# Hybrid encoder layer on one core: roots through memory, attention outputs one step later, another order in the MLP's head

## The chip, the core and the metric

The kernel runs on one core of a Trainium2 chip. Its time is the device time of one execution in microseconds (us). TensorE (PE) multiplies and transposes, VectorE (DVE), ScalarE (ACT) and GpSimd (POOL) do elementwise work, and transfers are issued from the queues of SyncE (SP) and ACT.

## The reference

The input is 1024 tokens by 1024 features. All arithmetic is in float32.

```python
hn = rmsnorm(h, norm_mix[l])
proj = jnp.einsum('bsd,de->bse', hn, w_in[l])
qa, ka, va, qb, kb, vb = jnp.split(proj, splits, axis=-1)
...
o_a = window_gqa_sink(qa, ka, va, sink[l])        # |i-j| <= 128, 8 heads, 2 key heads
o_b = neighbourhood_attention(qb, kb, vb, rpb[l]) # 8 x 16 windows on a 16 x 64 grid, 8 heads
mix = jnp.concatenate([rmsnorm(o_a, norm_a[l]), rmsnorm(o_b, norm_b[l])], axis=-1)
h = h + jnp.einsum('bse,ed->bsd', mix, w_out[l])
hn = rmsnorm(h, norm_ffn[l])
h = h + conv_gated_mlp(hn, w_gate[l], w_up[l], conv_w[l], conv_b[l], w_down[l])
return rmsnorm(h, norm_final)
```

## The kernel before

Features lie on the 128 partitions and tokens along the free dimension. Every float32 operand of a product is split into a rounded part (`hi`, made by ACT) and a remainder (`lo`, made by DVE as a subtraction), and a product is three matmuls: hi by hi, hi by lo, lo by hi. Roundings of weights are `whi` and `wlo`; of probabilities `ph` and `pl`; of the MLP's operands `hg`.

The program has four stretches. Up to about 57 us it computes the first three column tiles of the projection. Then two streams are interleaved by hand on PE: the attention's units (first 16 of the window attention, two groups of key heads times 8 blocks of tokens; then 32 of the grid attention, 8 heads times 4), and as filler the blocks of the remaining projections and of the first half of the output projection (`rest`, jobs 0 to 22, each of 16 blocks). A table of places, `aux[job, block]`, puts the norm of the first attention into the filler. After the attention come the second half of the output projection and the MLP, whose first four gate and up units ("the head") overlap the norm before it; then the rest of the MLP, the down product and the final norm.

PE's order is the order of the code. The order of the other engines is set by a list scheduler; `high_priority` pulls an instruction forward, and `behind(names)` keeps it after the last instruction that was recorded under these names: "high" is the latest `ph`, "rest" the latest `pl`, "narrow" the latest reciprocal of a norm.

Places that the change touches:

- `t_step` transposes probabilities into a bank `pt` and splits them; `v_step`, one step later, multiplies them with the values into the bank `o`. After the last one of a unit or of half a head, `leave` copies one half of the partitions of `o` into `ot` (ACT, L491 or L574) and adds it to the other half into `mix` (DVE, L495 or L576), at once.
- `square_a`, `narrow_a`, `wide_a`, `normed_a` are the norm of the first attention's output. `narrow_a` leaves 1024 reciprocal roots as `v`, 128 partitions by 8 columns. `wide_a`, at `aux[12, 11]` and `aux[12, 13]`, spreads each half of them over all partitions by four PE transposes (`widen`, L236) into a `pj` bank and copies it to `rstda` with ACT (L851). `normed_a` multiplies (DVE, L855, eight instructions).
- `OutA.run` adds the residual to a finished bank of the output projection (L659).
- In the MLP's head, `pure(f)` loads and rounds a gate weight, `settle_out` adds squares for the norm (L1069), and `head_weights(i, "s2")` forms a difference of weights (L1083). `p1`, `p2` and `p5` of a unit multiply into the banks `x`, `z` and `y`; a `join` (L1084) empties `z`. The units 2 and 3 use for `z` the two banks that the units 0 and 1 use for `y`.

Of the kernel before, what the change touches and what calls it, by code (L numbers as in the profile page):

```python
# [20 lines left out]
KT = D // 128  # L21
# [37 lines left out]
def hybrid_layer(tc, xT, w_first, w_in, w_out, w_gate, w_up, w_down, small, sink, rpb, consts, rope, out):  # L59
    nc = tc.nc  # L60
    with ExitStack() as ctx:
# [7 lines left out]
        tpool = inner("temps", 3)  # L69
        apool = inner("att", 2)  # L70
        spool = inner("stats", 6)

        slots = {"xg": 16, "op": 14, "mix": 8, "rstd": 1}

# [6 lines left out]
        def bank(name, tag):  # L81
            return psum.tile([128, HALF], F32, name=name, tag=tag)
# [319 lines left out]
                return lpool.tile([128, 2, 386], F32, name="p", tag="mix", bufs=slots["mix"], padded_shape=[128, 2, 512])  # L402
            return apool.tile([128, 2, 386], F32, name="p", tag="p", bufs=5, padded_shape=[128, 2, 392])

        deferred = []

        def exponentials(*order):
            while deferred:
                with tc.high_priority(offset=50):
                    deferred.pop(0)(*order)  # L410
# [39 lines left out]
        def unit_window(g, b):  # L450

            cs, n = near(b), 128 * len(near(b))
            ps4 = [None] * 4
            mask = w2(cst[:, K_MA + 128 * (cs[0] - b + 1):K_MA + 128 * (cs[-1] - b + 2)])
            st = {}

            def q_step(j):
                def go():
                    if j % 2 == 0:
                        st["p"] = pair_tile(True)  # L460
                    ps, _ = scores(qa[g, j // 2][j % 2], ka[g], b)
                    softmax(st, j % 2, ps, n, mask, nsink[:, 4 * g + j - j % 2:4 * g + j - j % 2 + 2])
                    ps4[j] = st["p"][:, j % 2, :]
                return go

            def t_step(i):
                def go():
                    if i == 0:
                        st["o"] = bank("o", "o")
                    pt = bank("pt", "pt")  # L470
                    for j in range(4):
                        nc.tensor.transpose(pt[:, j * 128:(j + 1) * 128], ps4[j][:, i * 128:(i + 1) * 128], ident)  # L472
                    ph, pl = split_pt(pt, HALF)
                    exponentials("high")

                    def v_step():
                        o, v = st["o"], va[g]
                        nc.tensor.matmul(o, v[:, cs[i], :], mv(ph[:, :]), start=i == 0, stop=False)
                        nc.tensor.matmul(o, v[:, cs[i], :], mv(pl[:, :]), start=False, stop=i == len(cs) - 1)
                        if i == len(cs) - 1:  # L480
                            leave()
                    return v_step
                return go

            def leave():
                ot = apool.tile([128, 2, 128], F32, name="ot", tag="ot", bufs=1, padded_shape=[128, 4, 128])
                o4 = pv(st["o"][:, :])
                halved = lambda ap: ap.rearrange("p (s w) -> p s w", s=2)
                for e in range(2):
                    me, other = slice(64 * e, 64 * e + 64), slice(64 - 64 * e, 128 - 64 * e)  # L490
                    nc.scalar.activation(ot[me].rearrange("p j (s w) -> p j s w", s=2), o4[other, e::2], AF.Copy)  # L491
                    for i in range(2):
                        if mix[2 * g + i] is None:
                            mix[2 * g + i] = big("mixa", "mix")
                        nc.vector.tensor_tensor(halved(mix[2 * g + i][me, b * 128:(b + 1) * 128]), o4[me, e + 2 * i], halved(ot[me, i, :]), op=ALU.add)  # L495

            return [q_step(j) for j in range(4)], [t_step(i) for i in range(len(cs))]

# [19 lines left out]
        def units_grid(h):  # L518
# [21 lines left out]
            def t_step(c):  # L540
                def go():
                    if c == 0:
                        st["o"] = [bank("o", "o") for _ in range(2)]
                    bs = near(c)
                    pt = bank("pt", "pt")
                    for i, b in enumerate(bs):
                        at = near(b).index(c) * 128
                        nc.tensor.transpose(pt[:, i * 128:(i + 1) * 128], ps4[b][:, at:at + 128], ident)
                    ph, pl = split_pt(pt, 128 * len(bs))

                    def v_step():
                        for half in range(2):
                            inb = [b for b in bs if b // 4 == half]
                            if not inb:
                                continue
                            lo, hi = (inb[0] - bs[0]) * 128, (inb[-1] - bs[0] + 1) * 128
                            dst = st["o"][half][:, (inb[0] % 4) * 128:(inb[-1] % 4 + 1) * 128]
                            final = c == (4 if half == 0 else NB - 1)
                            nc.tensor.matmul(dst, vb[h][:, c, :], mv(ph[:, lo:hi]), start=not st["begun"][half], stop=False, skip_group_check=True)
                            nc.tensor.matmul(dst, vb[h][:, c, :], mv(pl[:, lo:hi]), start=False, stop=final, skip_group_check=True)  # L560
                            st["begun"][half] = True
                            if final:
                                leave(half)
                    return v_step
                return go

            def leave(half):
                i = 4 + h // 2
                if mix[i] is None:
                    mix[i] = big("mixb", "mix")  # L570
                ot = apool.tile([128, HALF], F32, name="ot", tag="ot", bufs=1)
                w = lambda ap: ap.rearrange("p (b r c s) -> p b s r c", s=2, r=ROWS // 2, c=8)
                o = st["o"][half]
                nc.scalar.activation(ot[me], o[other], AF.Copy)  # L574
                dst = mix[i][me, :].rearrange("p (s r b c) -> p b s r c", s=2, b=NB, c=8)[:, 4 * half:4 * half + 4]
                nc.vector.tensor_tensor(dst, w(o[me, :]), w(ot[me, :]), op=ALU.add)  # L576

            chunks = [[0], [1, 2], [3, 4], [5, 6, 7]]
            return [([q_step(2 * i), q_step(2 * i + 1)], [t_step(c) for c in chunks[i]]) for i in range(4)]
# [56 lines left out]
        class OutA:  # L636
# [12 lines left out]
            def run(self):  # L649
                d = self.d  # L650
                h1[d] = big("h1", "mix" if d < 4 else "op")
                xt = tmp("xr")
                with behind(*["stacked"] * (d > 0)):
                    nc.sync.dma_start(xt, xT[d])
                for h in range(2):
                    ps = bank("pj", "pj")
                    yield from product(ps, self.w, mg[0:4], h)
                    with tc.high_priority(offset=500):
                        nc.vector.tensor_tensor(sv(h1[d][:, tsl(h)]), pv(ps[:, :]), sv(xt[:, tsl(h)]), op=ALU.add)  # L659

            def post(self):
# [180 lines left out]
                if h == 1:  # L842
                    inverse_root(norm["v"], 512)

        def wide_a(h):
            def go():
                if h == 0:
                    live["op"] += 1
                    norm["a"] = big("rstda", "op")
                with tc.high_priority(offset=500):  # L850
                    nc.scalar.activation(norm["a"][:, tsl(h)], widen(norm["v"][:, 4 * h:4 * h + 4], "pj"), AF.Copy)  # L851
            return go

        def normed_a(i, h):
            return lambda: nc.vector.scalar_tensor_tensor(  # L855
                mix[i][:, tsl(h)], mix[i][:, tsl(h)], col(C_NA + i), norm["a"][:, tsl(h)], op0=ALU.mult, op1=ALU.mult)

        aux[11, 8], aux[12, 2], aux[12, 5], aux[12, 11], aux[12, 13] = square_a, narrow_a, narrow_a, wide_a(0), wide_a(1)
        for i in range(8):
            aux[13, 1 + i + i // 2] = normed_a(*divmod(i, 2))  # L860
        aux[1, KEYS] = second_k
        filler = rest()
        live["op"] = sum(needs(m) for m in range(3))
# [102 lines left out]
            nc.scalar.activation(warm, eps, AF.Sqrt)  # L966
        fill(2)
        pend()


        last = tmp("sq")
# [75 lines left out]
        def operand(src, tag):  # L1047

            t = big("hg", tag, F32R)
            nc.scalar.activation(t[:, 0:HALF], src, AF.Copy)  # L1050
            nc.vector.tensor_tensor(t[:, HALF:S], src, f32(t[:, 0:HALF]), op=ALU.subtract)
            return t[:, 0:HALF], t[:, HALF:S]


# [5 lines left out]
        def settle_out():  # L1060
# [5 lines left out]
            with tc.high_priority(offset=500):  # L1066
                nc.scalar.activation(s2, at(d, h), AF.Square)
                if total[h] is not None:
                    nc.vector.tensor_tensor(s2, s2, total[h], op=ALU.add)  # L1069
            total[h] = s2  # L1070

        def normed(h, wide, ds):
# [16 lines left out]
        def head_weights(i, name):  # L1089
# [3 lines left out]
                nc.vector.tensor_tensor(t, u[:, 0:4], u[:, 4:8], op=ALU.add)  # L1093
            elif name == "s2":
                g = load_half(w_gate[f, :, 0:4])
                sub(t, t, g)
            elif name == "s4":
                g = load_half(w_gate[f, :, 4:8])
                sub(t, g, t)
# [170 lines left out]
        units = [Gated(f, *(("s", "o", "pj"), ("pj", "pt", "o"))[i // 2]) for i, f in enumerate(FO[:HEAD])]  # L1270
        units[0].p1()
        units[1].p1()
        pure(FO[2])
        units[0].p2()
        v = inverse_narrow([total[1]], D, "pt")
        units[1].p2()
        wide = widen(v, "pt")
        normed(1, wide, K1)
# [405 lines left out]
```

## Time and profile before

| | |
|---|---|
| median of three runs | 1016.34 us (1015.89 to 1016.55) |
| the profiled execution's own time | 1016.91 us |
| its span, first to last instruction | 1015.1 us |
| outside of the span | 1.8 us |
| granted TensorE clock | 0.998 |
| PE, DVE, ACT, POOL busy | 99%, 82%, 55%, 10% of the span |

The profiled execution is 0.57 us above the median. Busy shares are means over stretches of different kinds; PE's counts a matmul from its start to its modelled end, and matmuls overlap, so the distance between two starts is what a matmul costs in a dense stretch.

### The profile page before, as it was taken

The numbers are of one execution on the slowest core, as the hardware profiler recorded it, in microseconds if no ns is written. First come the engines' busy times: TensorE is split into PE (matmuls) and PEld (weight loads), VectorE is DVE, ScalarE is ACT, GpSimd is POOL, SyncE is SP. The second block draws the span as 40 slices with busy tenths as digits, with TensorE's granted clock in tenths as the row PEclk, the third lists the DMA queues.
The fourth block names the chain that finished last, engine by engine and source line by source line (L and its number), as shares of the span: only waits on it lengthen the run. The fifth ranks groups of instructions, "written<-read, shape, count | busy, mean of one in ns | idle before, by whom it ended". The sixth has DMA issues, their size and how long they took to land.

```text
span 1015.1 us, 14835 instructions
## 1 busy us (share of the span) xinstructions
PE 1006.3 (99%) x5086; PEld 890.2 (88%) x5086; DVE 832.7 (82%) x1566; ACT 561.8 (55%) x1081; POOL 104.0 (10%) x188
## 2 busy tenths in 40 slices
PE   9999999999999999999999999999999999999996
PEld 8899898899899888888888888888888888888886
DVE  7989887768888799999987786786777678986775
ACT  8567776658687554565544443444443645544451
POOL 0224342222232100000000000000000000000002
PEclk9999999999999999999999999999999999999999
DMA  8223122333334366231542233323232699866644
GB/s 295 83 74 92 34 73 63 83 83 83 84 93 135 126 203 222 73 104 63 203 180 100 98 115 114 104 94 131 88 135 88 227 345 322 297 226 231 226 153 166
DMA packets 68220, 144.94 MB, mean 143 GB/s; under 512 B 8240, under 2 KB 18736, under 8 KB 68144
## 3 DMA queue, kind: packets, MB, share of 16 engines
q1 hardware_dynamic: 58208, 118.88, 36.5%
q10 hardware_dynamic: 9936, 25.11, 6.4%
q8 instruction: 40, 0.66, 0.3%
q14 instruction: 36, 0.29, 0.1%
HBM read 103.58 MB, written 28.57 MB: 130 GB/s over the span
## 4 chain that ended last, share of the span: by engine, by line
PE 99%; DVE 1%; issue 0%; ACT 0%; DVEq 0%; POOL 0%; POOLq 0%
PE pj L179 8%; PE pj L181 8%; PE pj L180 8%; PE x L1045 7%; PE x L1043 7%; PE x L1044 7%; PE dn L1045 7%; PE dn L1044 7%; PE dn L1043 7%; PE s L393 4%; PE y L1045 4%; PE y L1043 4%; PE y L1044 4%; PE pt L472 2%; PE z L1043 2%; PE z L1045 2%
## 5 line engine op out<-in xcount | busy, mean ns | idle before, releaser
L1043 PE MATMUL x<-hg,whi 128*128 128x512 f32 x352 | 133.5, 379 | 0.0
L1044 PE MATMUL x<-hg,whi 128*128 128x512 f32 x352 | 133.4, 379 | 0.0
L1045 PE MATMUL x<-hg,wlo 128*128 128x512 f32 x352 | 133.4, 379 | 0.0
L1043 PE MATMUL dn<-xd,whi 128*128 128x512 f32 (+1 forms) x330 | 120.8, 366 | 0.0
L1044 PE MATMUL dn<-xd,whi 128*128 128x512 f32 (+1 forms) x330 | 120.5, 365 | 0.0
L1045 PE MATMUL dn<-xd,wlo 128*128 128x512 f32 (+1 forms) x330 | 120.5, 365 | 0.0
L1017 ACT ACTIVATE whi<-ws 128x512 fp32r<-128x512 f32 (+1 forms) x100 | 60.7, 621 | 74.1 <-DVE ws L1153 14.7
L432 ACT ACTIVATE p<-p,nm 128x385 f32<-128x385 f32 (+3 forms) x128 | 75.1, 587 | 47.0 <-DVE nm L424 44.1
L179 PE MATMUL pj<-xgh,whi 128*128 128x512 f32 x245 | 99.7, 407 | 0.1
L436 POOL TENSOR_SCALAR p<-p,sm 128x384 f32<-128x384 f32 (+1 forms) x128 | 75.6, 603 | 196.0 <-DVE sm L434 179.9
L180 PE MATMUL pj<-xgl,whi 128*128 128x512 f32 x245 | 92.9, 379 | 0.0
L181 PE MATMUL pj<-xgh,wlo 128*128 128x512 f32 x245 | 92.9, 379 | 0.0
L1017 ACT ACTIVATE whi<-raw 128x512 fp32r<-128x512 f32 (+1 forms) x102 | 60.9, 610 | 50.1 <-PE x L1044 15.4
L1018 DVE TENSOR_TENSOR wlo<-ws,whi 128x512 fp32r<-128x512 f32 (+1 forms) x100 | 66.7, 683 | 19.1 <-ACT whi L1017 18.8
L447 DVE TENSOR_TENSOR pl<-pt,ph 128x384 fp32r<-128x384 f32 (+2 forms) x108 | 63.3, 586 | 17.4 <-ACT ph L446 16.3
L1043 PEld LDWEIGHTS x<-hg,whi 128*128 128x128 f32 x352 | 66.5, 189 | 9.5
L1045 PEld LDWEIGHTS x<-hg,wlo 128*128 128x128 f32 x352 | 66.5, 189 | 9.4
L1044 PEld LDWEIGHTS x<-hg,whi 128*128 128x128 f32 x352 | 66.5, 189 | 9.4
L1504 POOL TENSOR_TENSOR h<-h,wide 128x256 f32<-128x256 f32 (+1 forms) x6 | 5.4, 916 | 669.8 <-ACT wide L1500 669.8
L1018 DVE TENSOR_TENSOR wlo<-raw,whi 128x512 fp32r<-128x512 f32 (+1 forms) x102 | 66.7, 670 | 7.0 <-ACT whi L1017 6.8
L446 ACT ACTIVATE ph<-pt 128x384 fp32r<-128x384 f32 (+2 forms) x108 | 55.3, 512 | 25.8 <-PE pt L472 14.4
L1045 PEld LDWEIGHTS dn<-xd,wlo 128*128 128x128 f32 x330 | 62.5, 189 | 7.7
(267 smaller groups left out, 2507.6 us busy)
## 6 DMA issues: line engine op xcount, KB each, us to landing
xd<-x SPq DMA_DIRECT2D x77, 256.0 KB, 4.9
raw<-in_w_down_dram SPq DMA_DIRECT2D x72, 256.0 KB, 4.5
raw<-in_w_gate_dram SPq DMA_DIRECT2D x22, 512.0 KB, 3.5
raw<-in_w_up_dram SPq DMA_DIRECT2D x22, 512.0 KB, 3.7
x<-c ACTq DMA_DIRECT2D x22, 512.0 KB, 2.8
raw<-in_w_in_dram SPq DMA_DIRECT2D x30, 256.0 KB, 2.7
raw<-in_w_down_dram SPq DMA_DIRECT2D x36, 192.0 KB, 4.4
x<-t ACTq DMA_DIRECT2D x11, 512.0 KB, 2.6
```

Source lines behind the costliest of these rows:

```text
L179: nc.tensor.matmul(ps, w[0], mv(x[0][:, tsl(h)]), start=first, stop=False)
L180: nc.tensor.matmul(ps, w[0], mv(x[1][:, tsl(h)]), start=False, stop=False)
L181: nc.tensor.matmul(ps, w[1], mv(x[0][:, tsl(h)]), start=False, stop=last)
L432: nc.scalar.activation(p[:, j, 0:e], p[:, j, 0:e], AF.Exp, bias=nm, scale=-1.0, accum_out=sm[:, j:j + 1])
L436: mark["scaled"] = nc.gpsimd.tensor_scalar(p[:, i, 0:m], p[:, i, 0:m], sm[:, i:i + 1], 1.0, op0=ALU.mult, op1=ALU.mult)
L446: mark["high"] = nc.scalar.activation(ph[:, 0:n], ps[:, 0:n], AF.Copy)
L447: mark["rest"] = nc.vector.tensor_tensor(pl[:, 0:n], ps[:, 0:n], f32(ph[:, 0:n]), op=ALU.subtract)
L1017: nc.scalar.activation(hi, src, AF.Copy)
L1018: nc.vector.tensor_tensor(lo, src, f32(hi[:, :, :]), op=ALU.subtract)
L1043: nc.tensor.matmul(ps, w[0], x[0], start=first and i == 0, stop=False, skip_group_check=True)
L1044: nc.tensor.matmul(ps, w[0], x[1], start=False, stop=False, skip_group_check=True)
L1045: nc.tensor.matmul(ps, w[1], x[0], start=False, stop=last and i == len(ws) - 1, skip_group_check=True)
```

## The change

The first attention's reciprocal roots no longer go through eight PE transposes. One transpose turns `v` into 8 rows of 128, ACT copies them out of the bank, a transfer writes them (4 KB) to a tile in device memory, and a second transfer, five blocks later in the code, reads them back into all 128 partitions of `rstda` (512 KB). Both are issued on ACT's queue. The eight multiplications move four blocks later, and each stays behind the latest `pl`.

`leave` is no longer called at once but put into a list, which the next `t_step` empties after it has split its probabilities, behind its "high" and "rest". `OutA`'s addition stays behind "rest" too.

In the MLP's head `pure(FO[2])` stands after `units[0].p2()` and the norm's root in the code, the differences "s2" stay behind "narrow", and the last addition of squares stays behind the latest rounding of an operand.

```diff
+        spread_pool = ctx.enter_context(tc.tile_pool(name="roots", bufs=1, space=bass.MemoryType.DRAM))
+        roots = spread_pool.tile([8, 128], F32, name="roots")
...
+        def leave_all(*order):
+            while leaving:
+                leaving.pop(0)(order)
...
                     exponentials("high")
+                    leave_all("high", "rest")
...
                         if i == len(cs) - 1:
-                            leave()
+                            leaving.append(leave)
...
-            def leave():
+            def leave(order):
...
+                with behind(*order):
+                    for e in range(2):
+                        me, other = slice(64 * e, 64 * e + 64), slice(64 - 64 * e, 128 - 64 * e)
+                        nc.scalar.activation(ot[me].rearrange("p j (s w) -> p j s w", s=2), o4[other, e::2], AF.Copy)
...
                     ph, pl = split_pt(pt, 128 * len(bs))
+                    leave_all("high", "rest")
...
-                                leave(half)
+                                leaving.append(lambda order, half=half: leave(half, order))
...
-                    with tc.high_priority(offset=500):
+                    with tc.high_priority(offset=500), behind("rest"):
                         nc.vector.tensor_tensor(sv(h1[d][:, tsl(h)]), pv(ps[:, :]), sv(xt[:, tsl(h)]), op=ALU.add)
...
-        def wide_a(h):
+        def row_a():
+            ps, row = bank("row", "pj"), norm["sq"][0:8, 0:128]
+            nc.tensor.transpose(ps[0:8, 0:128], norm["v"], ident)
+            with tc.high_priority(offset=500):
+                nc.scalar.activation(row, ps[0:8, 0:128], AF.Copy)
+                nc.scalar.dma_start(roots, row)
+
+        def wide_a():
+            live["op"] += 1
+            norm["a"] = big("rstda", "op")
+            with tc.high_priority(offset=500):
+                nc.scalar.dma_start(norm["a"], bass.AP(tensor=roots.tensor, offset=roots.offset, ap=[[0, 128], [1, S]]))
+
+        def normed_a(i, h):
             def go():
-                if h == 0:
-                    live["op"] += 1
-                    norm["a"] = big("rstda", "op")
-                with tc.high_priority(offset=500):
-                    nc.scalar.activation(norm["a"][:, tsl(h)], widen(norm["v"][:, 4 * h:4 * h + 4], "pj"), AF.Copy)
+                with behind("rest"):
+                    nc.vector.scalar_tensor_tensor(
+                        mix[i][:, tsl(h)], mix[i][:, tsl(h)], col(C_NA + i), norm["a"][:, tsl(h)], op0=ALU.mult, op1=ALU.mult)
...
-        aux[11, 8], aux[12, 2], aux[12, 5], aux[12, 11], aux[12, 13] = square_a, narrow_a, narrow_a, wide_a(0), wide_a(1)
+        aux[11, 8], aux[12, 2], aux[12, 5], aux[12, 10], aux[12, 15] = square_a, narrow_a, narrow_a, row_a, wide_a
         for i in range(8):
-            aux[13, 1 + i + i // 2] = normed_a(*divmod(i, 2))
+            aux[13, 5 + i + i // 2] = normed_a(*divmod(i, 2))
...
-            nc.vector.tensor_tensor(t[:, HALF:S], src, f32(t[:, 0:HALF]), op=ALU.subtract)
+            mark["operand"] = nc.vector.tensor_tensor(t[:, HALF:S], src, f32(t[:, 0:HALF]), op=ALU.subtract)
...
-                    nc.vector.tensor_tensor(s2, s2, total[h], op=ALU.add)
+                    with behind(*["operand"] * (h == 1 and d == KT - 1)):
+                        nc.vector.tensor_tensor(s2, s2, total[h], op=ALU.add)
...
-                sub(t, t, g)
+                with behind("narrow"):
+                    sub(t, t, g)
...
-        pure(FO[2])
         units[0].p2()
         v = inverse_narrow([total[1]], D, "pt")
+        pure(FO[2])
```

What the scheduler makes of it is seen at three places. The line numbers of the kernel after are higher by 2 to 20 for the same instruction.

On ACT, before, around the spreading of the roots (`v` is the root of the first attention's norm, `p` an exponential, `rstda` the spread roots):

```order
L432 ACTIVATE p,sm<-p,nm 128x256
L446 ACTIVATE ph<-pt 128x384
L432 ACTIVATE p,sm<-p,nm 128x384
L446 ACTIVATE ph<-pt 128x384
L171 ACTIVATE whi<-raw 128x512
L851 ACTIVATE rstda<-sw 128x512
L432 ACTIVATE p,sm<-p,nm 128x384
L851 ACTIVATE rstda<-sw 128x512
```

The same place after:

```order
L438 ACTIVATE p,sm<-p,nm 128x256
L452 ACTIVATE ph<-pt 128x384
L860 ACTIVATE sq<-row 8x128
L438 ACTIVATE p,sm<-p,nm 128x384
L861 DMA roots<-sq 8x128
L452 ACTIVATE ph<-pt 128x384
L173 ACTIVATE whi<-raw 128x512
L438 ACTIVATE p,sm<-p,nm 128x384
L867 DMA rstda<-roots 128x1024
L452 ACTIVATE ph<-pt 128x384
```

The two copies are replaced by a small one, one exponential earlier, and by two transfers, with a `ph`, a `whi` and an exponential between them; the next `ph` stands behind the second transfer.

On DVE, before, in the window attention at about 104 us (L424 is the masked score with its row maximum, two rows each; `t` is a projection's tile out of its bank):

```order
L447 TENSOR_TENSOR pl<-pt,ph 128x512
L434 RECIPROCAL sm<-sm 128x2
L424 ISA p,nm<-s,cst,nsink 128x256
L424 ISA nm 128x1
L495 TENSOR_TENSOR mixa<-o,ot 64x128 x2
L424 ISA p,nm<-s,cst,nsink 128x256
L424 ISA nm 128x1
L495 TENSOR_TENSOR mixa<-o,ot 64x128 x2
L247 TENSOR_TENSOR t<-pj,rstd_334 128x8x8x8
L447 TENSOR_TENSOR pl<-pt,ph 128x512
```

The same place after:

```order
L453 TENSOR_TENSOR pl<-pt,ph 128x512
L440 RECIPROCAL sm<-sm 128x2
L430 ISA p,nm<-s,cst,nsink 128x256
L430 ISA nm 128x1
L430 ISA p,nm<-s,cst,nsink 128x256
L430 ISA nm 128x1
L453 TENSOR_TENSOR pl<-pt,ph 128x512
L249 TENSOR_TENSOR t<-pj,rstd_337 128x8x8x8
```

The four additions into `mixa` that stood ahead of the second `pl` are gone from here; they follow later, behind a `pl`.

On DVE, before, in the MLP's head at about 411 us (L219 and L229 are the sum and the reciprocal of the second half's norm, L1084 the joins of the units 0 and 1):

```order
L1018 TENSOR_TENSOR wlo<-raw,whi 128x512 x2
L1083 TENSOR_TENSOR ws<-ws,raw 128x512 x2
L1084 TENSOR_TENSOR gs<-z,gs 128x512
L219 TENSOR_REDUCE v_5100<-ss 128x4
L1018 TENSOR_TENSOR wlo<-raw,whi 128x512
L229 RECIPROCAL v_5100<-v_5100 128x4
L1084 TENSOR_TENSOR gs<-z,gs 128x512
```

The same place after:

```order
L1037 TENSOR_TENSOR wlo<-raw,whi 128x512 x2
L1104 TENSOR_TENSOR gs<-z,gs 128x512
L221 TENSOR_REDUCE v_5086<-ss 128x4
L1037 TENSOR_TENSOR wlo<-raw,whi 128x512
L231 RECIPROCAL v_5086<-v_5086 128x4
L1103 TENSOR_TENSOR ws<-ws,raw 128x512 x2
L1104 TENSOR_TENSOR gs<-z,gs 128x512
```

Two differences "s2" moved from ahead of the norm's sum to behind its reciprocal, ahead of the second join here; the other two, which had stood 29 rows ahead of this place, went to the same place by that order, and the pair that stood here to one 29 rows behind it. The roundings `wlo` stand where they stood.

More of the change, by code (lines that the diff above doesn't have):

```diff
@@ L403, in pair_tile @@
             return apool.tile([128, 2, 386], F32, name="p", tag="p", bufs=5, padded_shape=[128, 2, 392])
-        deferred = []
+        deferred, leaving = [], []
+        def leave_all(*order):
+            while leaving:
+                leaving.pop(0)(order)
         def exponentials(*order):
@@ L488, in leave @@
                 halved = lambda ap: ap.rearrange("p (s w) -> p s w", s=2)
[L489 to L495, printed above, removed]
+                for i in range(2):
+                    if mix[2 * g + i] is None:
+                        mix[2 * g + i] = big("mixa", "mix")
+                with behind(*order):
+                    for e in range(2):
+                        me, other = slice(64 * e, 64 * e + 64), slice(64 - 64 * e, 128 - 64 * e)
+                        nc.scalar.activation(ot[me].rearrange("p j (s w) -> p j s w", s=2), o4[other, e::2], AF.Copy)
+                        for i in range(2):
+                            nc.vector.tensor_tensor(halved(mix[2 * g + i][me, b * 128:(b + 1) * 128]), o4[me, e + 2 * i], halved(ot[me, i, :]), op=ALU.add)
             return [q_step(j) for j in range(4)], [t_step(i) for i in range(len(cs))]
@@ L562, in v_step, with leave @@
                             if final:
-                                leave(half)
+                                leaving.append(lambda order, half=half: leave(half, order))
                     return v_step
                 return go
-            def leave(half):
+            def leave(half, order):
                 i = 4 + h // 2
@@ L573, in leave @@
                 o = st["o"][half]
-                nc.scalar.activation(ot[me], o[other], AF.Copy)
                 dst = mix[i][me, :].rearrange("p (s r b c) -> p b s r c", s=2, b=NB, c=8)[:, 4 * half:4 * half + 4]
-                nc.vector.tensor_tensor(dst, w(o[me, :]), w(ot[me, :]), op=ALU.add)
+                with behind(*order):
+                    nc.scalar.activation(ot[me], o[other], AF.Copy)
+                    nc.vector.tensor_tensor(dst, w(o[me, :]), w(ot[me, :]), op=ALU.add)
             chunks = [[0], [1, 2], [3, 4], [5, 6, 7]]
@@ L968, in hybrid_layer @@
         pend()
+        leave_all()
         last = tmp("sq")
```

3 lines of the change are left out of this document (removed).

## The prediction

> **What bounds the kernel now.** I read the waits of PE first, because PE is busy for 99% of the span.
>
> ```profile
> PE warm_ps L148 <- POOL eps L143: 1.0, 1, 1.0
> PE sw L236 <- DVE v L229: 0.6, 1, 0.6
> ```
>
> These are the two largest sums; the first is the start of the program. Busy time by windows says the same of the attention, and shows the only loose stretch:
>
> ```profile
> 60.00:210.00 150.00, 150.00 (x858) 134.64 (x856) 128.06 (x368) 108.46 (x275) 49.80 (x101) 1.00 0.29 75
> 990.00:1015.00 25.00, 17.39 (x153) 16.84 (x150) 13.77 (x30) 4.72 (x11) 5.36 (x6) 0.91 0.46 169
> ```
>
> In the first window PE is busy for 150.00 of 150.00 us. DVE has 128.06 and ACT 108.46: much, but less. The change does not touch the last window. Since records of matmuls overlap, a busy PE can hide short waits, so I read the chain that ended last and PE's starts in the timeline.
>
> ```profile
> 256.29 0.61 DVE v L206
> 256.94 0.48 PE pj L179
> ...
> 261.44 0.44 PE sw L236 x4
> 263.88 0.46 PE sw L236 x4
> ```
>
> The chain stays on PE through the attention, with rare steps to DVE such as this `v`, and it holds both groups of transposes that spread the first attention's roots. So the time is PE's list of work plus a few short waits. A change gains only what it takes out of that list or out of those waits; it loses only where another engine gets so late that PE runs dry.
>
> **Transposes.** Eight `sw` transposes go, one `row` transpose comes. PE's order is otherwise the same. Two readings of their price:
>
> ```profile
> 260.94 0.49 PE L548 MATMUL pt<-cst,p 128*128 128x128 f32 x3
> 261.27 0.60 PE L236 MATMUL sw<-cst,v 128*128 128x128 f32 x4
> ```
>
> ```profile
> L236 PE MATMUL sw<-cst,v 128*128 128x128 f32 x42 | 6.3, 274 | 0.8 <-DVE v L229 0.6
> ```
>
> One record lasts 274 ns, but the three `pt` start 0.33 us ahead of the next group: 0.11 each. The chain gives the two groups 0.44 and 0.46, together 0.90. I take starts, since the records overlap. The new transpose costs between 0.11 (a start distance) and 0.27 (a whole record); by the starts I take 0.12, and 0.90 − 0.12 is **0.78 us** off PE's path (0.63 at the other end). It has no cover, as PE works without a pause there.
>
> By the Trainium skill ("TensorE: Matmul & The Clock Gate", Part 4: PE-mode transpose) a 128x128 transpose costs about 275 ns in a kernel's context. The record's 274 agrees, the starts do not; a sum by that figure is the rival R4.
>
> **Attention outputs.** `ot` and the additions into `mix` only move, one step later and behind `ph` and `pl`. On DVE that takes four half-width additions, or one wide one, from ahead of a `pl` for which PE waits:
>
> ```profile
> 104.53 0.50 DVE L495 TENSOR_TENSOR mixa<-o,ot 64x128 f32<-64x128 f32 x2 [0.34 <-ACT ot L491]
> ...
> 105.67 0.68 DVE L447 TENSOR_TENSOR pl<-pt,ph 128x512 fp32r<-128x512 f32 x1
> ```
>
> ```profile
> 106.41 0.48 PE L479 MATMUL o<-pl,v 128*128 128x512 f32 x1
> 106.73 0.27 PE L472 MATMUL pt<-cst,p 128*128 128x128 f32 x1
> ```
>
> ```profile
> 333.43 0.33 PE L559 MATMUL o<-ph,v 128*128 128x384 f32 x1
> 333.75 0.43 PE L560 MATMUL o<-pl,v 128*128 128x384 f32 x1
> 334.02 0.38 PE L179 MATMUL pj<-mgh,whi 128*128 128x512 f32 x1
> ```
>
> ```profile
> 425.88 0.38 PE L1045 MATMUL z<-hg,wlo 128*128 128x512 f32 x1
> 426.10 0.38 PE L1043 MATMUL y<-hg,whi 128*128 128x512 f32 x1
> ```
>
> The last pair gives the dense step, 0.22 us for 512 columns; for 384 three quarters of that are 0.165. Then the matmul at 106.41 loses 0.32 − 0.22 = 0.10, those at 333.43 and 333.75 lose 0.32 − 0.165 = 0.155 and 0.27 − 0.165 = 0.105. Together 0.36, with rounding **0.4 us**, is what late `pl` costs PE in the places where I can see it right behind an output's addition. The `pl` at 105.67 has 0.50 of additions and 0.34 of their wait directly ahead, more than the 0.10 lost, so the loss goes entirely. The other stall in the chain, at 256.94, waits for a `v` of the norm and stays. Bounds: nothing, if the loss re-forms at the next step, and 0.4.
>
> What is late next is the bank `o`. It is emptied one step later; the next writer of the same bank comes a whole unit or half a head later, which the instructions in between fill with several us of PE's work. `OutA`'s addition, behind `pl` now, is 1.0 to 1.2 us later by the order and DVE's durations; its bank is asked for again a half of a product later, twelve matmuls of 0.22 or 2.6 us. Both are covered, at a price of nothing; were the cover gone, the excess over it would be the cost.
>
> **Roots through memory.** On ACT two copies go and a small one and two issues come:
>
> ```profile
> 260.77 0.62 ACT L432 ACTIVATE p<-p,nm 128x384 f32<-128x384 f32 x1 [0.23 <-DVE nm L424]
> ...
> 263.93 0.62 ACT L432 ACTIVATE p<-p,nm 128x384 f32<-128x384 f32 x1 [0.91 <-DVE nm L424]
> ...
> 264.55 0.58 ACT L851 ACTIVATE rstda<-sw 128x512 f32<-128x512 f32 x1
> 265.42 0.49 ACT L446 ACTIVATE ph<-pt 128x384 fp32r<-128x384 f32 x1 [0.29 <-PE pt L548]
> ```
>
> By the order the write is issued behind the exponential of 260.77, so about 261.4, and the read behind the one of 263.93, so about 264.6, where the second copy (0.58) stood. ACT is in order: if the roots have not landed by 264.6, the read's wait holds ACT, and the `ph` of 265.42 is queued behind it. That `ph` can be late by some time, because PE asks for it here:
>
> ```profile
> 266.78 0.22 PE L559 MATMUL o<-ph,v 128*128 128x128 f32 x1
> ```
>
> With 0.49 for `ph`, it may start at 266.29: a landing up to 4.9 us after 261.4 costs PE nothing. No row shows a 4 KB write from eight partitions. The nearest are the sixteen writes of 256 KB on this same queue (the first answer below), a 4 KB load, and for the read the 512 KB loads (name, queue, count, size, median us to landing):
>
> ```profile
> DMA to landing us min/median/max: 2.0/3.7/4.9
> ```
>
> ```profile
> x<-c ACTq DMA_DIRECT2D x22, 512.0 KB, 2.8
> ...
> xt<-in_xT_dram SPq DMA_DIRECT2D x6, 512.0 KB, 8.6
> ...
> par<-in_small_dram ACTq DMA_DIRECT2D x1, 4.0 KB, 3.0
> ```
>
> I take 2.0 to 3.0 us for the write: the fastest of the large writes, since it carries a sixty-fourth of their bytes, and the load of its size. The ends are 2.0 and, by the slowest load, 8.6. It lands at 263.4 to 264.4, ahead of the read's turn: price nothing. The read lands 2.8 to 8.6 after 264.6, at 267.4 to 273.2. The first multiplication asks for it eight blocks after the second group of `sw`; the two groups, two blocks apart, started 2.44 us apart in the chain, so that is 263.88 + 4 × 2.44 = 273.6. The slowest row would just do. The eight multiplications themselves only move.
>
> By the Trainium skill ("DMA: Bandwidth & Descriptors", Anatomy of one DMA) the fixed cost of a transfer, there for the GpSimd path, is about 2.0 us, mostly the receipt of the write, which "can cause a surprisingly long delay especially when the write target is HBM". The minimum here, 2.0, agrees; by it the read would wait for nothing, and the warning speaks for R2.
>
> **MLP's head.** Four "s2" differences move on DVE, in two pairs. The roundings `wlo` do not move by the order, so the third part does only some of what it says.
>
> ```profile
> 411.83 1.30 DVE L1083 TENSOR_TENSOR ws<-ws,raw 128x512 f32<-128x512 f32 x2
> 413.03 0.70 DVE L1084 TENSOR_TENSOR gs<-z,gs 128x512 f32<-128x512 f32 x1
> ...
> 424.86 0.69 DVE L1084 TENSOR_TENSOR gs<-z,gs 128x512 f32<-128x512 f32 x1
> ```
>
> The pair of 411.83 leaves the path to the norm's root, which had kept PE waiting 0.6 at most (the second row of the waits). Its place is taken by the pair from further ahead, behind the reciprocal; and a pair, 1.2 us (413.03 − 411.83), comes ahead of the join of 424.86. That join ends at 425.55, and its bank is the one that the `y` of 426.10 writes: 0.55 us of slack. I take nothing for both: root earlier by 1.2 can gain up to 0.6, a join later by 1.2 can cost 1.2 − 0.55 = 0.65.
>
> **The sum.** The profiled execution took 1016.91 us, 1015.1 of it span. 1016.91 − 0.78 − 0.4 = 1015.73. It lies 0.57 above the median of the runs, so the forecast for the median is 1016.34 − 1.18 = 1015.16, **1015.1 us**.
>
> **The rivals.** R1: leaving the outputs later only shifts the stalls, because DVE has the same work in a stretch where it is busy for 85%. For it: no instruction goes from DVE there. Against: PE waits only behind the clusters. Then only the transposes count: 1016.34 − 0.78 = 1015.6.
>
> R2, the other side: the write's receipt is late, the read's wait holds ACT, and `ph` queues behind it. It decides from a landing 4.9 us after the issue. At the far end of the rows, 8.6, PE waits 3.7 us once: 1015.1 + 3.7 = 1018.8. For it: the order puts one `ph` right behind the read. Against: writes sixty-four times as large land within 4.9.
>
> R3: in the MLP's head the pair ahead of the join costs 0.65 and the root gives nothing: 1015.1 + 0.65 = 1015.8. For it: DVE is dense from 411 to 425. Against: DVE's four differences are only reordered, so an earlier idle place may give the time back.
>
> R4, faster: a transpose blocks PE for its whole record. Seven fewer are 7 × 0.274 = 1.92, and 1016.34 − 1.92 − 0.4 = 1014.0. Against it stand the starts 0.11 apart.
>
> **How the numbers follow.** Chances: the forecast 0.45, R1 0.20, R3 0.11, R2 0.12, R4 0.12. A measurement of this kernel can tell about 0.2%, 2.03 us, from no change: the bounds are 1014.31 and 1018.37. Forecast, R1 and R3 lie within them; R4 is faster, R2 slower at its far end, and a part of R2 stays inside. That gives faster 0.13, same 0.77, slower 0.10. The range reaches down to R4, 1014.0, and up past R3 into the first half of R2, 1017.0; what it leaves out is the rest of R2, with the edge of R4.
>
> **What would show it.** Right: in the new timeline the blocks at 261 and 264 follow the `pt` without `sw`; 106.41 and 333.43 are followed at the dense step; ACT's wait ahead of the read is nothing and the `ph` behind it starts by its `pt`. R2 shows as PE idle at an `o` with `ph` as its releaser, just behind the roots. R3 shows as a `y` that waits for a `gs`. The forecast is wrong if PE's waits in the attention or the head grow by over 1 us in sum, or if the places of the removed transposes gain far more or less than 0.8.

## The result and the profile after

The kernel after takes 1017.61 us (median of 21 runs, 1017.13 to 1018.23), the kernel before 1016.34 us (21 runs, 1015.44 to 1016.89): 1.27 us more, a ratio of 1.0013 with a 95% interval of 1.0007 to 1.0018. The forecast was 1015.1, the range 1014.0 to 1017.0. The profiled execution of after has a span of 1015.6 us.

The waits of PE, of the kernel after:

```profile
PE pj L181 <- DVE v L208: 1.7, 1, 1.7
PE warm_ps L150 <- POOL eps L145: 1.0, 1, 1.0
PE sw L238 <- DVE v L231: 0.6, 1, 0.6
PE ss L226 <- ACT s L1543: 0.6, 1, 0.6
PE pj L181 <- DVE t L249: 0.4, 1, 0.4
```

The first and the last row are new. Both are a projection's matmul that waits for its bank: once until the sum of the first attention's norm (`v`, L208) has read the transposed squares out of it, once until a projection's tile (`t`, L249) is out.

To see where time goes I laid PE's starts of the same matmul in the two traces beside each other, after minus before, and took the growth of the difference over a stretch. Up to 60 us executions differ by about 1 us with the same code there, and at 103.5 before's profile has about 0.2 that no other trace of this case has. The ledger leaves both out and begins at 104 us (us of before's profile):

| stretch | after | what stands there |
|---|---|---|
| 104-110 | -0.17 | stalls behind late `pl` gone, 106.41 among them |
| 110-255 | +0.07 | |
| 255-259 | +1.65 | the wait for `v` |
| 259-270 | -0.73 | eight transposes out, one in |
| 270-281 | -0.42 | small stalls of before gone |
| 281-300 | +0.66 | the wait for `t` |
| 300-331 | +0.01 | |
| 331-345 | -0.27 | stalls behind late `pl` gone |
| 490-505 | +0.28 | MLP, behind the head |
| sum | +1.08 | measured +1.27 between the medians |

A ledger compares one execution of each kernel, and the 21 executions of after alone spread over 1.1 us, so a sum of it meets the medians to a few tenths at best.

First the wait for `v`. DVE's timeline, before and then after, from the first `kb` of a key tile to the sum:

```profile
253.35 0.80 DVE L576 TENSOR_TENSOR mixb<-o,ot 64x512 f32<-64x512 f32 x1
254.08 0.73 DVE L303 SCALAR_TENSOR_TENSOR kb<-t,cst,ka 128x512 fp32r<-128x512 f32 x1
...
255.55 0.74 DVE L303 SCALAR_TENSOR_TENSOR kb<-t,cst,ka 128x512 fp32r<-128x512 f32 x1
256.22 0.67 DVE L206 TENSOR_REDUCE v<-ss 128x4 f32<-128x512 f32 x1
```

```profile
253.45 1.03 DVE L305 SCALAR_TENSOR_TENSOR kb<-t,cst,ka 128x512 fp32r<-128x512 f32 x1
...
255.21 0.82 DVE L587 TENSOR_TENSOR mixb<-o,ot 64x512 f32<-64x512 f32 x1
255.95 1.39 DVE L305 SCALAR_TENSOR_TENSOR kb<-t,cst,ka 128x512 fp32r<-128x512 f32 x1
257.27 0.67 DVE L208 TENSOR_REDUCE v<-ss 128x4 f32<-128x512 f32 x1
```

The same instructions stand ahead of the sum, in another order: the addition into `mixb` moved from ahead of both `kb` to between them. The two `kb` take 1.03 and 1.39 us in place of 0.73 and 0.74, 0.95 more. GpSimd's timeline of after (its bias differences `xb` for a grid head, and scalings of `p` ahead of them), and PE's:

```profile
252.51 1.43 POOL L442 TENSOR_SCALAR p<-p,sm 128x384 f32<-128x384 f32 x2 [5.71 <-DVE sm L440]
255.37 1.42 POOL L521 TENSOR_TENSOR xb<-cst,rr 128x384 f32<-128x384 f32 x1 [1.43 <-DVE nm L430]
256.75 1.16 POOL L522 TENSOR_TENSOR xb<-cst,rr 128x256 f32<-128x256 f32 x1
```

```profile
258.00 0.48 PE L181 MATMUL pj<-xgh,whi 128*128 128x512 f32 x1 [1.71 <-DVE v L208]
```

Both long `kb` start while GpSimd is at work. Before, the second `kb` started at 255.55, ahead of GpSimd's difference, which came here; the second row is the same difference for the next grid head, with no `kb` beside it:

```profile
255.71 1.43 POOL L512 TENSOR_TENSOR xb<-cst,rr 128x384 f32<-128x384 f32 x1 [1.87 <-DVE nm L424]
...
278.77 0.98 POOL L512 TENSOR_TENSOR xb<-cst,rr 128x384 f32<-128x384 f32 x1 [1.46 <-DVE nm L424]
```

The difference takes 0.98 to 1.00 in the five other grid heads from 186 us on, before and after. So the collision costs GpSimd some 0.44 as well, before (where `kb` was first) and after (where GpSimd was). The same score (`nm`) frees both, so who is first is decided by whether `kb` stands right behind it. Then the wait for `t`, on DVE and on PE:

```profile
284.13 0.73 DVE L872 SCALAR_TENSOR_TENSOR mixa<-mixa,par,rstda 128x512 f32<-128x512 f32 x1
...
285.71 0.75 DVE L872 SCALAR_TENSOR_TENSOR mixa<-mixa,par,rstda 128x512 f32<-128x512 f32 x1
286.38 0.69 DVE L249 TENSOR_TENSOR t<-pj,rstd 128x512 f32<-128x512 f32 x1
```

```profile
287.12 0.48 PE L181 MATMUL pj<-xgh,whi 128*128 128x512 f32 x1 [0.40 <-DVE t L249]
```

Two moved multiplications stand ahead of a tile that before began to leave its bank at 285.07 (DVE's timeline, before):

```profile
285.07 0.68 DVE L247 TENSOR_TENSOR t<-pj,rstd 128x512 f32<-128x512 f32 x1
```

What the prediction's rows turned into: the roots' transpose in the chain, both transfers on ACT's queue with the `ph` behind the read, and the `o` at 333.

```profile
261.19 0.11 PE row L858
```

```profile
261.89 0.54 ACTq L861 DMA_DIRECT2D roots<-sq  x1
...
264.46 0.35 ACTq L867 DMA_DIRECT2D rstda<-roots  x1
...
265.68 0.49 ACT L452 ACTIVATE ph<-pt 128x384 fp32r<-128x384 f32 x1 [0.65 <-PE pt L557]
```

```profile
334.00 0.33 PE L569 MATMUL o<-ph,v 128*128 128x384 f32 x1
334.16 0.33 PE L570 MATMUL o<-pl,v 128*128 128x384 f32 x1
334.32 0.38 PE L181 MATMUL pj<-mgh,whi 128*128 128x512 f32 x1
```

The transpose costs 0.11. The read was issued at 264.46, so the write had landed by then, in under 2.6 us (the issue waited for nothing); the `ph` waited for its `pt`, not behind ACT. The `o` follow each other at 0.16.

### The profile page after: what moved, and what is told of

Read it like the earlier page. It is cut to its first block, busy times and chain, and to the rows that moved or that the text cites. A ratio compares the mean times of both kernels' runs of the same rounds, so it can differ in the third digit from the quotient of the medians.

```text
span 1015.6 us, 14814 instructions
## 1 busy us (share of the span) xinstructions
PE 1004.9 (99%) x5079; PEld 889.5 (88%) x5079; DVE 832.0 (82%) x1566; ACT 561.0 (55%) x1080; POOL 107.0 (11%) x188
## 4 chain that ended last, share of the span: by engine, by line
PE 96%; DVE 2%; ACT 1%; issue 1%; POOL 0%; DVEq 0%; POOLq 0%
PE pj L181 8%; PE pj L183 8%; PE pj L182 8%; PE x L1062 8%; PE x L1063 7%; PE x L1064 7%; PE dn L1064 7%; PE dn L1062 7%; PE dn L1063 7%; PE y L1064 4%; PE y L1063 4%; PE y L1062 4%; PE s L395 3%; PE pt L478 2%; PE z L1064 2%; PE z L1063 2%
## 5 line engine op out<-in xcount | busy, mean ns | idle before, releaser
L442 POOL TENSOR_SCALAR p<-p,sm 128x384 f32<-128x384 f32 (+1 forms) x128 | 78.8, 628 | 196.1 <-DVE sm L440 176.8
L1063 PEld LDWEIGHTS dn<-xd,whi 128*128 128x128 f32 x330 | 62.5, 189 | 7.7
L1062 PEld LDWEIGHTS dn<-xd,whi 128*128 128x128 f32 x330 | 62.5, 189 | 7.7
```

The lines of the kernel that those rows point to most:

```text
L442: mark["scaled"] = nc.gpsimd.tensor_scalar(p[:, i, 0:m], p[:, i, 0:m], sm[:, i:i + 1], 1.0, op0=ALU.mult, op1=ALU.mult)
L1062: nc.tensor.matmul(ps, w[0], x[0], start=first and i == 0, stop=False, skip_group_check=True)
L1063: nc.tensor.matmul(ps, w[0], x[1], start=False, stop=False, skip_group_check=True)
```

## The experiments

In the expectations A and B are the theories named there. Medians are of 11 runs each (21 for after, beside 1016.34); the kernel before had 1016.48 to 1016.50 beside them. The ledger is made as above.

| kernel | us | ratio to before, 95% | 104-110 | 255-259 | 259-281 | 281-345 | 490-505 |
|---|---|---|---|---|---|---|---|
| after | 1017.61 | 1.0013 (1.0007 to 1.0018) | -0.17 | +1.65 | -1.15 | +0.40 | +0.28 |
| e1, leaving late alone | 1017.64 | 1.0012 (1.0003 to 1.0021) | -0.17 | +1.62 | -0.34 | -0.21 | 0.00 |
| e2, roots alone | 1016.77 | 1.0002 (0.9993 to 1.0011) | -0.17 | -0.08 | -1.14 | +1.66 | 0.00 |
| e3, head alone | 1016.60 | 1.0002 (0.9993 to 1.0011) | 0.00 | -0.12 | -0.04 | -0.01 | +0.29 |
| e4, GpSimd's order | 1017.22 | 1.0009 (1.0000 to 1.0017) | -0.17 | +1.38 | -1.14 | +0.38 | +0.28 |
| e5, one output at once | 1016.43 | 0.9998 (0.9990 to 1.0007) | -0.17 | +0.61 | -1.15 | +0.39 | +0.28 |
| e6, one output two steps late | 1016.15 | 0.9996 (0.9987 to 1.0005) | -0.17 | +0.42 | -1.15 | +0.40 | +0.28 |
| e7, early multiplications | 1017.38 | 1.0008 (0.9999 to 1.0017) | -0.17 | +1.61 | -1.14 | -0.10 | +0.29 |
| e8, e6 and e7 without the head | 1015.84 | 0.9993 (0.9984 to 1.0002) | -0.17 | +0.42 | -1.14 | +0.03 | 0.00 |
| e9, roots, early multiplications | 1015.61 | 0.9991 (0.9983 to 1.0000) | -0.02 | -0.13 | -1.14 | +0.33 | 0.00 |
| e10, e9 and late leaving from the 4th head | 1015.22 | 0.9988 (0.9979 to 0.9997) | -0.07 | -0.14 | -1.14 | -0.09 | 0.00 |

**e1, e2, e3: the three parts alone.** Each is the kernel before with one part of the diff.

> The kernel before with the second part alone: attention outputs one step later, and the output projection's addition behind the latest pl. Theory A (the 1.7 us wait of PE for the norm's sum v at 258.0 comes from this part, which moves an addition between the two kb of a key tile): that wait is here, 1.4 to 1.7 us, the stalls near 104-107 and at 333 are gone (-0.33 and -0.24), sum +0.9, so about 1017.2 us. Rival B (the wait comes from the roots' way through memory): no wait over 0.4 us in the attention, 1016.3 - 0.6 = 1015.8 us.

> The kernel before with the first part alone: roots through memory, multiplications four blocks later and behind the latest pl. Theory A: the transposes give -0.71, the stalls at 274-279 that stood behind the old multiplications -0.45, and the multiplications now stand ahead of a projection's evacuation near 286, +0.6; no wait for v at 258. Sum -0.5, about 1015.8 us. Rival B: the wait of 1.7 us for v is here, and the time is 1017 us or more.

> The kernel before with the third part alone, the order in the MLP's head. Theory A: the attention is as before, and the list scheduler's new order reaches past the head into the MLP, where one x waits some 0.3 us near 498; about 1016.6 us. Rival B (this part changes nothing that PE sees): 1016.3 us, no wait at 498.

The wait for `v` is in e1 and in neither of the others: it comes from leaving late (A); e1's 1017.64 is 0.4 above the time that A had, and its profiled execution has a stall of 0.31 at 700-820 that after's has not. The transposes' 0.73 is in e2 and not in e1 or e3. The order of the MLP's head costs 0.29 near 498 wherever it is in, and nothing inside the head. Two things were not expected. The stall at 106.41, where before's `pt` starts 0.32 behind the `o`, is not in e2 either, although the additions stand there as before. The same pair in e2, then in e3:

```profile
105.39 0.38 PE L481 MATMUL o<-pl,v 128*128 128x512 f32 x1
105.61 0.60 PE L474 MATMUL pt<-cst,p 128*128 128x128 f32 x4
```

```profile
105.77 0.48 PE L479 MATMUL o<-pl,v 128*128 128x512 f32 x1
106.09 0.60 PE L472 MATMUL pt<-cst,p 128*128 128x128 f32 x4
```

These start 0.22 and 0.32 apart. Of the five kernels whose window attention leaves at once, before, e3 and e9 have 0.32 in their profiled execution, e10 0.27 and e2 0.22; all seven that leave late there (after, e1, e4 to e8) have 0.22. So late leaving goes with the dense step every time, and the old order does not show the stall in every execution. Also, e2 loses 1.66 from 281 to 345, more than after does there (the row is the waits of PE in e2, two `o` that wait for `pl`):

```profile
PE o L562 <- DVE pl L449: 0.6, 2, 0.3
```

So the first part costs more there where outputs leave at once (e9 shows below that it is the place of the multiplications), and e2's expected 1015.8 was 1.0 too low. The three medians' differences from before, 1.15, 0.28 and 0.11, add to 1.54, after has 1.27.

**e4, e5, e6: what makes `v` late.** e4 changes GpSimd's order alone:

```diff
+                nc.gpsimd.tensor_tensor(xv[:, 0::4], mk[:, 0::4], view(-1, 2, 2), op=ALU.subtract)
                 nc.gpsimd.tensor_tensor(xv[:, 1:4], mk[:, 1:4], view(-1, 1, 3), op=ALU.subtract)
-                nc.gpsimd.tensor_tensor(xv[:, 0::4], mk[:, 0::4], view(-1, 2, 2), op=ALU.subtract)
```

> The kernel after with one edit: GpSimd's two differences that make the bias tile xb of a head stand in the other order, the short one (0.72 us) ahead of the long one (1.42 us). No other engine's order changes. Theory A (VectorE's kb near 256 takes 1.39 in place of 0.74 us because it stands still until GpSimd's difference, begun before it, has ended): kb takes 0.8 to 0.95, the wait of PE for v falls from 1.7 to about 1.1, time 1017.0 us. Rival B (kb is long, or v late, for another reason): kb 1.4, wait 1.7, 1017.6 us.

The second `kb` and what GpSimd did at that time, in e4:

```profile
256.63 1.12 DVE L305 SCALAR_TENSOR_TENSOR kb<-t,cst,ka 128x512 fp32r<-128x512 f32 x1
257.68 0.67 DVE L208 TENSOR_REDUCE v<-ss 128x4 f32<-128x512 f32 x1
```

```profile
256.05 1.16 POOL L521 TENSOR_TENSOR xb<-cst,rr 128x256 f32<-128x256 f32 x1 [1.43 <-DVE nm L430]
```

With no change on DVE, `kb` fell from 1.39 to 1.12 and the wait from 1.65 to 1.38. The short difference took 1.16 here and not 0.72, so the effect is half of what I expected. Idle time ahead of it is not the reason: in another head of e4 it stands behind 2.61 us of idle time and takes 0.72:

```profile
209.77 0.72 POOL L521 TENSOR_TENSOR xb<-cst,rr 128x256 f32<-128x256 f32 x1 [2.61 <-DVE nm L430]
```

The collision drew it out by 0.44, as it did the long one in after. Its end fits: in after GpSimd's first difference ends at 255.37 + 1.42 = 256.79 and the sum behind `kb` starts 0.48 later; here it ends at 257.21 and the sum starts 0.47 later. `kb` waits for GpSimd.

e5 and e6 move one output, the second half of the third grid head, in the kernel after (`leave_all` of e6 empties only what stood in the list when it began):

```diff
+                                if (h, half) == (2, 1):
+                                    leave(half, ())                                                   # e5
+                                    leaving.append(lambda order: leaving.append(lambda order: leave(1, order)))   # e6
...
```

> The kernel after, with one attention output (the second half of the third grid head) left at once, as in the kernel before; all others stay one step later. VectorE's order there becomes addition, pl, score, kb, kb, norm's sum: the addition stands ahead of both kb again, but the two kb now stand together behind the score whose end also lets GpSimd's bias difference start. Theory A (GpSimd's difference holds the second kb): the pair takes 2.1 us or more in place of 1.4, the wait for v stays at 1.2 to 1.7, time 1017.3 us. Rival B (the wait comes from the addition's place alone): wait 0.3 as before, 1016.2 us.

> The kernel after, with the same one output left two steps later. VectorE's order becomes pl, score, kb, norm's sum, and the addition comes behind. The second kb can start before GpSimd's difference does. Theory A: kb 0.75, the sum about 0.9 us earlier or more, PE's wait for v 0.2 to 0.5 in place of 1.7, time 1016.3 us. Rival B (PE's wait is set by something else that is late there): wait over 1.2, 1017.6 us.

DVE and GpSimd in e5, then DVE in e6:

```profile
254.89 1.40 DVE L305 SCALAR_TENSOR_TENSOR kb<-t,cst,ka 128x512 fp32r<-128x512 f32 x2
256.22 0.68 DVE L208 TENSOR_REDUCE v<-ss 128x4 f32<-128x512 f32 x1
```

```profile
255.05 2.07 POOL L521 TENSOR_TENSOR xb<-cst,rr 128x384 f32<-128x384 f32 x1 [1.12 <-DVE nm L430]
```

```profile
255.27 0.74 DVE L305 SCALAR_TENSOR_TENSOR kb<-t,cst,ka 128x512 fp32r<-128x512 f32 x1
256.01 0.17 DVE L440 RECIPROCAL sm<-sm 128x2 f32<-128x2 f32 x1
256.10 0.67 DVE L208 TENSOR_REDUCE v<-ss 128x4 f32<-128x512 f32 x1
```

In e5 theory A had the roles wrong: the pair of `kb` took 1.40, undisturbed, and GpSimd's difference 2.07 in place of 0.98. It ended at 257.12, and 0.98 ahead of that is 256.14, about the end of the pair (256.29): GpSimd's work came behind both `kb`. So the two do exclude each other, but here DVE held on and GpSimd waited; PE's wait was 0.7, and the time, 1016.43, was nearer to what B had. e6 came out as A had it: `kb` 0.74, the sum 1.17 us earlier, 1016.15. In both the ledger keeps 0.4 to 0.6 at this place, without a delayed second `kb` (in e6 the first `kb` still takes 1.03 beside GpSimd's scaling of `p`, which can be up to 0.29 of it). So of the 1.65, some 1.0 to 1.2 is the order of this one addition with the collision, and 0.4 to 0.6 is the rest of leaving late.

Where that rest comes from the trace of after suggests: the addition of the half before (DVE's timeline, after) fell from 244.72 to 247.29, behind a hole in which DVE waited for ACT.

```profile
244.90 1.53 DVE L198 TENSOR_TENSOR sq<-sq 128x512 f32<-128x512 f32 x2 [0.36 <-ACT sq L196]
...
247.29 0.82 DVE L587 TENSOR_TENSOR mixb<-o,ot 64x512 f32<-64x512 f32 x1
```

From there DVE works on to the tile `t` of 249.24, from which ACT makes `ka` and the exponentials. e10, in which this addition too is at once, has -0.14 at 255-259; that fits, but this one addition was not tried by itself.

**e7 to e10: the multiplications, and a faster version.** e7 and the later ones put the multiplications back at their old places. e10 also has the window attention's outputs at once, and sorts the grid's by head:

```diff
-            aux[13, 5 + i + i // 2] = normed_a(*divmod(i, 2))
+            aux[13, 1 + i + i // 2] = normed_a(*divmod(i, 2))
```

```diff
+                                if h < 3:
+                                    leave(half, ())
+                                else:
+                                    leaving.append(lambda order, half=half: leave(half, order))
```

> The kernel after, with the eight multiplications by the roots at their old places in the code, four blocks earlier, the roots still through memory. Theory A (the 0.4 us wait at 287.1 comes from two late multiplications ahead of a projection's evacuation): that wait goes, -0.6; the read landed at 268.4, ahead of the first multiplication, so nothing waits for it; some of the stalls at 274 to 279 (0.45 in the kernel before) come back. 1017.1 to 1017.5 us. Rival B: the multiplications wait for the read, and v-steps behind them wait for pl: over 1018 us.

> The kernel after without its third part (the MLP's head in the order of before), with the one output two steps later and the multiplications four blocks earlier. Theory A: transposes -0.7, the stalls at 258, 287 and 498 gone: 1015.4 us, faster than both. Rival B (the two changes of place bring new waits of the same size): 1016.3 us or more.

> The kernel before with the first part alone, and with the multiplications kept at their old places in the code (still behind the latest pl). Theory A (the new waits of PE near 286, 328 and 333 in the first part alone come from multiplications that stand four blocks later): they go, and the gain of 0.73 from the transposes and 0.4 at 274 to 279 stays: 1015.3 us. Rival B (they come from the transfers or from the order behind pl): the waits stay, 1016.7 us.

> As the run before, and attention outputs one step later only in the grid heads behind the third (the window attention and the first three grid heads leave at once, as before), with the output projection's addition behind the latest pl. Theory A (one step later is worth 0.2 to 0.3 us at 333 and costs only where kb and GpSimd's difference meet, near 256): no wait for v, 0.25 off the stalls at 333, 1015.1 us. Rival B (one step later brings new waits wherever it is): 1015.5 us or more.

e7: the 0.66 at 281-300 is gone (0.00), and the gain at 270-281 stays, where I expected part of it to be lost; the one at 331-345 falls from 0.27 to 0.09. The read takes 3.9 us to land, from 264.46 to 268.4; that is early enough. The median fell by 0.23 only; the profiled execution of e7 lost 0.64 at 700-820, where PE waits for a rounding in the down product, which e1 (0.31) and e3 (0.15) show too and the others do not. e8 and e9 are not told from before by their intervals, which reach 1.0002 and 1.0000, and e8's 1015.84 lies between its A and its B. e9 loses 0.31 more than before at 331-345, and e10, late from the fourth head on, 0.09 less than before. e10 is faster than both kernels: 1015.22 us, 1.26 below before. Its DVE at the place of the wait:

```profile
255.09 0.74 DVE L305 SCALAR_TENSOR_TENSOR kb<-t,cst,ka 128x512 fp32r<-128x512 f32 x1
255.76 0.68 DVE L208 TENSOR_REDUCE v<-ss 128x4 f32<-128x512 f32 x1
```

## Why the prediction was wrong

**Transposes: right.** 0.73 in all kernels with this part (0.78 forecast). R4, which took the whole record of 274 ns, is out.

**Attention outputs: the gain right, the failing step beside it.** The stalls behind late `pl` went as forecast: 0.17 at 104-110 and 0.27 at 331-345 in after, together 0.44 for 0.36. The step that failed is "What is late next is the bank `o`" and the price of nothing put on it. I asked which buffer the late addition itself would hold, and not which instructions would now stand beside others: the addition, put between the two `kb`, moved the second `kb` behind the start of GpSimd's difference. GpSimd's timeline was not read at all. Leaving late cost 1.65 us at this place (e1), more than all gains of the forecast, 1.18; 1.0 to 1.2 of it goes when this one addition is moved (e5, e6), and e4 moves it by 0.27 from GpSimd's side alone.

The trace of before held the price. Two of the attention's sixteen `kb` of this size begin inside one of GpSimd's records, and they take 1.01 and 0.96 us; the other fourteen take 0.74 on average. Of `wlo`, also with two operands in SBUF, 13 begin inside (57 to 345 us) and take 0.86 on average, up to 1.05, and 18 outside, 0.69; `pl` of 384 columns, with one operand in a bank, takes 0.55 in both cases. The Trainium skill ("SBUF — State Buffer", section "SBUF: two separate sides") says that DVE and GpSimd share a port pair as an exclusive lock, taken for the whole instruction by whichever starts first, and that DVE needs it for two inputs from SBUF. After and e4 agree in that `kb` waits (1.39 and 1.12 for 0.74). Two things do not follow from it: in e5 GpSimd's instruction was recorded as begun at 255.05, between the starts of the two `kb`, and the second `kb` still went first; and in after and e4 GpSimd's difference, recorded as begun 0.58 ahead of `kb`, was itself drawn out by 0.44. No run here shows why.

**Roots through memory: the transfer right, the multiplications wrong.** The write landed in time, R2 did not occur, and the read was early. But "the eight multiplications themselves only move" was priced at nothing, without asking what stood where they went: two stand ahead of a tile's evacuation (its copy out of the bank), 0.66 us in after (e7 against after), and 1.66 in e2 with other stalls to 345. On the other side 0.42 at 270-281, which I had not counted, went too; since e1, with the multiplications in place, shows 0.34 there, it is not theirs alone.

**MLP's head.** The head itself moved by nothing, as forecast, and R3 did not occur. But the order changes past the head: the scheduler gave DVE another order in the MLP behind it, and a weights' difference came ahead of a join (497.75 and 498.35), so that one `x` starts 0.40 behind the matmul ahead of it and not 0.22, which e3 shows with this part alone. DVE before, DVE after, and PE after:

```profile
496.52 1.27 DVE L1218 SCALAR_TENSOR_TENSOR cv<-gs,par,cv 128x1023 f32<-128x1023 f32 x1
497.71 0.68 DVE L1084 TENSOR_TENSOR c<-x,c 128x512 f32<-128x512 f32 x1
```

```profile
497.75 0.69 DVE L1182 TENSOR_TENSOR ws<-raw,ws 128x512 f32<-128x512 f32 x1
498.35 0.69 DVE L1104 TENSOR_TENSOR c<-x,c 128x512 f32<-128x512 f32 x1
```

```profile
498.69 0.38 PE L1064 MATMUL y<-hg,wlo 128*128 128x512 f32 x1
499.09 0.48 PE L1062 MATMUL x<-hg,whi 128*128 128x512 f32 x1
```

**The rivals.** R1 came nearest, in that stalls re-form elsewhere, but it had them at the size of what went. No rival had a mechanism that costs more than the change gains in the attention. Still open: why e2 loses 0.54 at 320-331 and e9 does not, the small stall of 0.25 to 0.27 at 410-430 in e8 and e9, the stall at 700-820 in e1, e3 and e7, the rest of 0.4 to 0.6 in e5 and e6, and what the output projection's addition behind the latest `pl` is worth, which no run changed by itself.

## What to carry to other kernels

When a list scheduler moves an instruction, look at its new neighbours on all engines, GpSimd too. Here an instruction with two operands in SBUF went ahead of GpSimd's while it stood right behind the score that freed GpSimd; with one instruction put between, it waited until GpSimd's record had ended. Moving work away from where it stands late is only half of the account; name what comes to stand behind it at its new place, above all evacuations of banks for which PE will ask. A stall of 0.1 us can be missing from one execution and be there in the next: read it in several executions before it enters a sum, or is struck from one.

## What was not expected of the hardware

GpSimd and DVE exclude each other in either direction: the same bias difference delayed a `kb` from 0.74 to 1.39 us in after, and in e5 was itself drawn out from 0.98 to 2.07 us by two `kb` that follow each other. Where GpSimd's record begins ahead of `kb` (after, e1, e4), the sum behind `kb` starts 0.47 to 0.48 us behind the end of that record, and GpSimd's own difference takes 0.44 longer than without a `kb` beside it.
